# A hybrid encoder block on one Trainium2 core: two own buffers for the raw LoRA tile, and the first MLP slice's sums and squares on other engines

## The chip, the core and the metric

The kernel runs on one core of a Trainium2 chip. A core has five engines that run side by side and wait for each other through semaphores: TensorE (PE in the profile; its weight loads are shown apart as PEld), VectorE (DVE), ScalarE (ACT), GpSimd (POOL) and SyncE (SP). Each takes its instructions in a fixed order. Transfers between the chip's main memory and the on-chip memory (SBUF) are issued from the queue of an engine; in the kernel before, only SyncE and ScalarE issue any. TensorE writes to PSUM, from where VectorE and ScalarE read.

The metric is the time of one execution in microseconds (us). The kernel before has a median of 891.74 us over three runs (891.09 to 892.44). One execution was profiled; it took 891.46 us, and its span from the first to the last instruction is 889.7 us.

## What is computed

One layer of a streaming encoder, for 512 tokens and 16 learned meta tokens ahead of them, width 1024, all in float32:

```python
u = rmsnorm(h, norm_mix)
proj = u @ w_in
y_rw = rwkv7_branch(proj[..., :C_RW], ...)
y_fx = fox_branch(proj[..., C_RW:C_RW + C_FX], ...)
gates = sigmoid(proj[..., C_RW + C_FX:] + b_gate)
merged = gates[..., :1024] * (y_rw @ w_out_rw) + gates[..., 1024:] * (y_fx @ w_out_fx)
h = h + merged @ w_o
z = rmsnorm(h, norm_mlp)
h = h + square(relu(z @ w_up)) @ w_down
```

`rwkv7_branch` is a recurrence over the tokens; two of its inputs, the decay and the gate, go through small LoRA products (`w_lora_up`, `a_lora_up`, `g_lora_up`). `fox_branch` is causal attention with a forget gate. The MLP has 4096 hidden channels.

## The kernel before

**Precision.** A float32 operand is split into a high half (`whi`, a cast on ScalarE) and a low half (`wlo`, the difference, on VectorE or GpSimd), and each product is three passes: high by high, high by low, low by high. So every weight that is loaded costs a cast and a subtraction before TensorE can use it. `load_h` (lines 228 to 236) and `split` (268 to 270) do this; the raw weight tile `wraw`, `whi` and `wlo` have four buffers each, which is two blocks of weights.

**Who sets the order.** TensorE's order in the mixer (the recurrence, the attention and the input projections) is made by `Turns` and `Clock` (lines 62 to 183): several streams of work, each step with the time at which a cost model expects its inputs; the first stream that can go on is taken, and TensorE's instructions are kept in that order. The order of the other engines' instructions, and of the transfers in each queue, is made by the framework's own planner: it goes by the order of the program (work of the most urgent streams ahead of the rest) and by the times at which its cost model expects each instruction's inputs and buffers. On the chip, each queue is then worked off strictly in that order, whenever the inputs really come.

**The mixer** (up to about 450 us of the span) first loads the transposed input in two halves of four pieces (`xt`, lines 337 to 341), squares and sums it on TensorE (lines 351 to 359), and projects. Four pairs of heads follow. `load_lora` (lines 667 to 672) is called eight times: for each pair once in `decay` (line 699, part 0), and once at the start of each of the two `chain` streams per pair (line 887, part 1, used later in `group_norm`). It loads a raw tile `lraw`, 128 by 128, and splits it into `lw`. `lraw` carries the tag `yT`: it takes turns in one single buffer with `rkb` (line 764), `tmp` of the triangular inverse (line 829) and `yT` of the group norm (line 968).

**Between** lie the output projections, the residual, the second norm and the transposes of `z` (lines 1033 to 1131, until about 558 us).

**The MLP** runs in four slices of four channel pairs (`SLICES`, `FIRST`). In each slice:
- The up projection: 8 blocks of 24 matmuls (`up_part`, line 1139). After each block `up_evac` (line 1146) takes it out of PSUM: ScalarE computes `r = relu(po)`, VectorE `max(po, 0) * r`, which is the square. After every second block `left_factors` (line 1152) makes the seven left factors of a Strassen-Winograd product in `R`, each as a high half `fhi` (ScalarE) and a low half `flo` (VectorE).
- The right factors: for each pair, `factor_sums` (line 1179) loads four quarters of the down weight (`quarter`, line 1174, tile `traw` with three buffers, from SyncE's queue) and adds them on GpSimd to four sums T1 to T4; T2 needs T1, and T4 needs T2. The other three right factors are quarters themselves, loaded as `wraw`.
- Seven products (`product`, line 1240) of the left with the right factors, whose results VectorE and ScalarE add up. `fill` (line 1190) prepares the halves of the right factors ahead of them.

The first slice differs in its start: its first three blocks go in two halves of the tokens (lines 1214 to 1223), since the second half of `z` comes later.

Of the kernel before, what the change touches and what calls it, by code (L numbers as in the profile page):

```python
# [9 lines left out]
F32 = mybir.dt.float32  # L10
# [3 lines left out]
AF = mybir.ActivationFunctionType  # L14
ALU = mybir.AluOpType
# [171 lines left out]
def kernel(ctx, tc, ht, x, win, par, cst, gain, lora, wout, wo, wup, wdn, out, dbg=None):  # L187
    nc = tc.nc
    dbg = dbg or {}
    mm = nc.tensor.matmul  # L190
    act = nc.scalar.activation
    V, G, A = nc.vector, nc.gpsimd, nc.scalar
# [45 lines left out]
    def load_w(src, low=(V, V)):  # L238

        return [load_h(src[:, 512 * j:512 * j + 512], low[j], "w", (4, 4, 4)) for j in range(2)]  # L240
# [27 lines left out]
    def split(hi, lo, x):  # L268
        A.copy(hi, x)  # L269
        V.tensor_tensor(lo, x, hi.bitcast(F32), ALU.subtract)  # L270
# [6 lines left out]
    quarters = [[wdn[i][256 * c:256 * c + 256] for c in range(8)] for i in range(4)]  # L277

    with ExitStack() as st:
# [28 lines left out]
        rp = st.enter_context(tc.tile_pool(name="rp", bufs=1))  # L308
# [356 lines left out]
            return t[:, PADT:]  # L665

        def load_lora(p, part, bufs):
            raw = rp.tile([128, 128], F32, name="lraw", tag="yT")
            nc.sync.dma_start(raw, lora[p][:, 128 * part:128 * part + 128])
            lw = [wp.tile([128, 128], F32R, name=f"lw{part}{i}", bufs=bufs) for i in range(2)]  # L670
            split(lw[0], lw[1], raw)
            return lw
# [211 lines left out]
        def chain(g, prs):  # L884

            y = y_rw[:, 2 * g:2 * g + 2, :].rearrange("p a (b c) -> p a b c", c=64)
            lws = [load_lora(2 * g + pr_, 1, 2) for pr_ in range(2)]

            def ppy(name):
# [149 lines left out]
    def ppo():  # L1039
        return ps.tile([128, 512], F32, name="po")  # L1040
# [4 lines left out]
    with ExitStack() as st:  # L1045
# [7 lines left out]
        for m in range(KB):  # L1053
            w = load_w(wout[m])
            pp = []
            for br in range(2):
# [3 lines left out]
                po = ppo()  # L1060
# [21 lines left out]
        for j in range(2):  # L1082
            we = yp.tile([128, 2, 2, 512], F32R, name=f"we{j}", tag=("y_rw", "y_fx")[j])
            for x in range(2):
                raw = wp.tile([128, 512], F32, name="wraw", bufs=4)
# [11 lines left out]
        for k in range(KB):  # L1097
            raw = wp.tile([128, 512], F32, name="wraw", bufs=4)
# [9 lines left out]
        for i in range(4):  # L1108
            po = ppo()
# [26 lines left out]
    with ExitStack() as st:  # L1136
        dp = st.enter_context(tc.tile_pool(name="dp", bufs=1))

        def up_part(w, po, t0, t1):
            n = 0  # L1140
            for k in range(KB):
                for a, b in passes(wk(w, k), Z):
                    mm(po[:, t0:t1], a, b[:, k, t0:t1], start=n == 0, stop=n == 23)  # L1143
                    n += 1

        def up_evac(po, out):

            r = dp.tile([128, 512], F32, name="r", bufs=2)
            act(r, po, AF.Relu)
            V.scalar_tensor_tensor(out, po.rearrange("p (a b) -> p a b", b=256), 0.0, r.rearrange("p (a b) -> p a b", b=256), ALU.max, ALU.mult)  # L1150

        def left_factors(fhi, flo, j, R):

            def halves(a, b):
                A.copy(fhi[:, j, a:b], R[:, a:b])
                V.tensor_tensor(flo[:, j, a:b], R[:, a:b], fhi[:, j, a:b].bitcast(F32), ALU.subtract)

            halves(0, 3)
            a11, a12, s1, s2, s4 = (R[:, i, :] for i in (A11, A12, S1, S2, S4))
            V.tensor_tensor(R[:, S3:S1 + 1, :], R[:, 0:3:2, :], bc(R[:, 7, :], 1, 2), ALU.subtract)  # L1160
            V.tensor_tensor(s2, a11, s1, ALU.add)  # L1161
            V.tensor_tensor(s4, s2, a12, ALU.subtract)  # L1162
            halves(3, 7)

        A11, A12, A22, S3, S1, S2, S4 = range(7)
        B11, B12, B22, B21, T1, T2, T3, T4 = range(8)
# [4 lines left out]

        sums = {}

        def quarter(right, pair, pool=dp, name="traw", bufs=3):
            raw = pool.tile([128, 512], F32, name=name, bufs=bufs)
            nc.sync.dma_start(raw, quarters[right][pair // 2][128 * (pair % 2):128 * (pair % 2) + 128])
            return raw

        def factor_sums(p0, j):
            pair = p0 + j  # L1180
            b11, b12, b22, b21 = (quarter(x, pair) for x in (B11, B12, B22, B21))
            for x, c, d in (T1, b11, b12), (T3, b12, b22), (T2, T1, b22), (T4, T2, b21):
                t = dp.tile([128, 512], F32, name=f"t{x}{j}")
                G.tensor_tensor(t, sums[c, pair] if c in (T1, T2) else c, d, ALU.add)  # L1184
                sums[x, pair] = t

        def right_factor(right, pair):
            return sums[right, pair] if (right, pair) in sums else quarter(right, pair, wp, "wraw", 4)

        def fill(n):  # L1190

            while line and len(ready) < n:
                right, p, j = line.pop(0)
                raw = right_factor(right, p + j)
                hi = wp.tile([128, 512], F32R, name="whi", bufs=4)
                lo = wp.tile([128, 512], F32R, name="wlo", bufs=4)
                split(hi, lo, raw)
                ready.append((hi, lo))
# [10 lines left out]
        for p0, n_pairs in zip(FIRST, SLICES):  # L1209
# [3 lines left out]
            held, R = [], None  # L1213
# [6 lines left out]
            for n, b_ in enumerate(blocks):  # L1220
                if held:
                    w, po = held.pop(0)
                    up_part(w, po, 256, 512)
                else:
                    w = load_w(wup[b_])
                    po = ppo()
                    up_part(w, po, 0, 512)
                if n == 2 * n_pairs - 1:
                    fill(AHEAD)
                if n % 2 == 0:  # L1230
                    R = yp.tile([128, 8, 256], F32, name="R", tag=("y_rw", "y_fx")[n // 2 % 2])
                    up_evac(po, R[:, 0:8:7, :])
                else:
                    up_evac(po, R[:, 1:3, :])
                    left_factors(fhi, flo, n // 2, R)
                    factor_sums(p0, n // 2)

# [149 lines left out]
```

## Time and profile before

| | |
|---|---|
| median of three runs | 891.74 us (891.09 to 892.44) |
| profiled execution | 891.46 us |
| its span | 889.7 us |
| TensorE busy | 855.4 us, 96% of the span |
| VectorE, ScalarE, GpSimd busy | 632.1, 447.9, 246.0 us |
| mean TensorE clock granted | 0.987 of full speed |
| data moved | 95.90 MB, a mean of 108 GB/s |

How to read the rows in the next parts. A row of a group names line, engine, operation, `output<-inputs`, their shapes and the count; then busy time and mean ns of one; then the idle time of the engine just before these instructions, and after each `<-` what ended most of it. A row in order of time begins with start and duration in us; several instructions of one kind in a row are merged into one (`x2`), and the bracket holds the idle time before. A row of waits has the waiting engine and line, then who released it, and the total in us, the number of waits and the longest. A row of windows begins with the stretch and its length in us, then the busy time of PE, PEld, DVE, ACT and POOL with their counts, then the granted TensorE clock, the share of the transfer engines in use and GB/s; where a window is asked for one engine or one line, only its busy time is there. A queue of transfers is written SPq; its rows are the issues, not the transfers. TensorE's ends are modelled, so that its idle time is good to some hundredths of a microsecond.

### The profile page before, as it was taken

The page shows a single profiled execution, that of the slowest core. Times are in us where ns is not written, and L with a number is a line of the kernel's source. Part 1 is how long each engine was busy: PE and PEld are TensorE (multiplying, and loading weights), DVE is VectorE, ACT ScalarE, POOL GpSimd, SP SyncE. Part 2 cuts the span into 40 slices and gives each one's busy share as a digit, 9 for nine tenths or more (in the row PEclk, how much of TensorE's full clock was granted, in tenths as well). Part 3 has the DMA queues.
Part 4 walks back from the last instruction along what each step waited for, and adds up shares of the span by engine and source line. Part 5 has one row for each costly group of instructions (what it writes and reads, how often), then busy time and mean ns, then how long its engine had stood idle before and what let it go on. Part 6 is the DMA issues. An engine that isn't in the chain of part 4 may idle for free. (4 is left out here: it accounts for less than half of the span.)

```text
span 889.7 us, 15657 instructions
## 1 busy us (share of the span) xinstructions
PE 855.4 (96%) x5896; PEld 697.0 (78%) x5896; DVE 632.1 (71%) x1178; ACT 447.9 (50%) x927; POOL 246.0 (28%) x201
## 2 busy tenths in 40 slices
PE   7889899999999999999979999999999999999998
PEld 6878887778896787677758778978888888888886
DVE  6975896547878883565467655598687768877787
ACT  7747333865465533664464553246445434543552
POOL 1154443222353351112102200550640152046000
PEclk9999999999999999999979999999999999999999
DMA  6121114021121241212266550463564175326431
GB/s 215 52 93 48 49 39 150 2 89 56 51 65 52 65 137 56 78 50 72 65 220 196 183 180 11 131 193 91 171 209 108 51 230 159 118 70 226 117 97 71
DMA packets 52363, 95.90 MB, mean 108 GB/s; under 512 B 5816, under 2 KB 6968, under 8 KB 52288
## 3 DMA queue, kind: packets, MB, share of 16 engines
q1 hardware_dynamic: 49984, 90.71, 33.0%
q10 hardware_dynamic: 2304, 4.20, 1.3%
q8 instruction: 46, 0.75, 0.4%
q14 instruction: 29, 0.24, 0.1%
HBM read 88.57 MB, written 6.31 MB: 107 GB/s over the span
## 5 line engine op out<-in xcount | busy, mean ns | idle before, releaser
L497 PE MATMUL pj<-uhi,whi 128*128 128x264 f32 (+1 forms) x480 | 167.3, 348 | 0.0
L497 PE MATMUL pj<-ulo,whi 128*128 128x264 f32 (+1 forms) x480 | 155.6, 324 | 2.4 <-DVE ulo L400 2.4
L467 POOL TENSOR_TENSOR wlo<-wraw,whi 128x512 fp32r<-128x512 f32 x76 | 104.7, 1381 | 191.4 <-ACT whi L466 175.0
L497 PE MATMUL pj<-uhi,wlo 128*128 128x264 f32 (+1 forms) x480 | 155.2, 323 | 0.0
L497 PEld LDWEIGHTS pj<-uhi,whi 128*128 128x128 f32 x480 | 91.4, 191 | 20.4 <-issue 11.3
L1184 POOL TENSOR_TENSOR t<-traw 128x512 f32<-128x512 f32 x32 | 47.0, 1478 | 209.1 <-DVE wlo L270 132.0
L497 PEld LDWEIGHTS pj<-ulo,whi 128*128 128x128 f32 x480 | 91.8, 191 | 7.2 <-DVE ulo L400 2.9
L497 PEld LDWEIGHTS pj<-uhi,wlo 128*128 128x128 f32 x480 | 91.6, 191 | 7.1
L1143 PE MATMUL po<-zhi,wlo 128*128 128x512 f32 (+1 forms) x248 | 95.0, 383 | 1.6 <-DVE wlo L235 1.6
L235 DVE TENSOR_TENSOR wlo<-wraw,whi 128x512 fp32r<-128x512 f32 x88 | 75.8, 874 | 27.7 <-ACT whi L234 27.7
L1143 PE MATMUL po<-zhi,whi 128*128 128x512 f32 (+1 forms) x248 | 94.8, 382 | 0.0
L1143 PE MATMUL po<-zlo,whi 128*128 128x512 f32 (+1 forms) x248 | 94.8, 382 | 0.0
L234 ACT CAST whi<-wraw 128x512 fp32r<-128x512 f32 x88 | 53.5, 618 | 46.3 <-DMA wraw<-in_wup 27.8
L466 ACT CAST whi<-wraw 128x512 fp32r<-128x512 f32 x80 | 49.0, 619 | 41.3 <-PE pj L497 21.0
L1256 PE MATMUL po<-wlo,fhi 128*128 128x512 f32 x160 | 62.8, 392 | 0.2 <-DVE wlo L270 0.2
L1256 PE MATMUL po<-whi,flo 128*128 128x512 f32 x160 | 62.5, 390 | 0.0
L270 DVE TENSOR_TENSOR wlo<-t,whi 128x512 fp32r<-128x512 f32 x64 | 49.3, 784 | 18.5 <-ACT whi L269 17.6
L269 ACT CAST whi<-t 128x512 fp32r<-128x512 f32 x64 | 40.0, 625 | 44.1 <-DVE wlo L270 19.8
L1256 PE MATMUL po<-whi,fhi 128*128 128x512 f32 x160 | 62.0, 389 | 0.0
L1143 PEld LDWEIGHTS po<-zhi,wlo 128*128 128x128 f32 x248 | 46.6, 188 | 11.4 <-DVE wlo L235 2.4
L1143 PEld LDWEIGHTS po<-zlo,whi 128*128 128x128 f32 x248 | 46.6, 188 | 9.1
L1143 PEld LDWEIGHTS po<-zhi,whi 128*128 128x128 f32 x248 | 46.6, 188 | 8.9
(294 smaller groups left out, 1842.2 us busy)
## 6 DMA issues: line engine op xcount, KB each, us to landing
wraw<-in_win SPq DMA_DIRECT2D x84, 256.0 KB, 2.8
wraw<-in_wup SPq DMA_DIRECT2D x64, 256.0 KB, 3.6
traw<-in_wdn SPq DMA_DIRECT2D x64, 256.0 KB, 3.0
wraw<-in_wdn SPq DMA_DIRECT2D x48, 256.0 KB, 2.7
gd<-gt ACTq DMA_DIRECT2D x16, 256.0 KB, 2.0
wraw<-in_wout SPq DMA_DIRECT2D x16, 256.0 KB, 3.1
gl<-gd SPq DMA_DIRECT2D x16, 256.0 KB, 3.0
wraw<-in_wo SPq DMA_DIRECT2D x16, 256.0 KB, 3.0
```

The costliest lines, as they stand in the source:

```text
L234: A.copy(hi, raw)
L235: low.tensor_tensor(lo, raw, hi.bitcast(F32), ALU.subtract)
L269: A.copy(hi, x)
L270: V.tensor_tensor(lo, x, hi.bitcast(F32), ALU.subtract)
L466: A.copy(hi, raw)
L467: low.tensor_tensor(lo, raw, hi.bitcast(F32), ALU.subtract)
L497: mm(po, a, b[:, k, a0:a1], start=n == 0, stop=n == 23)
L1143: mm(po[:, t0:t1], a, b[:, k, t0:t1], start=n == 0, stop=n == 23)
L1184: G.tensor_tensor(t, sums[c, pair] if c in (T1, T2) else c, d, ALU.add)
L1256: mm(x[i], a[:, k, left, 128 * i:128 * i + 128], c, start=start and k == 0 and n == 0, stop=stop and k == n_pairs - 1 and n == 2)
```

## The change

The parts are these:
- `lraw` no longer shares the buffer of `yT`. It has two buffers of its own.
- `up_evac` gets a switch. In the first slice (`p0 == 0`) the square is computed on ScalarE from `r`; in the others on VectorE as before.
- `factor_sums` adds on VectorE in the first slice and loads its quarters from GpSimd's queue; in the other slices it adds on GpSimd and loads from SyncE's queue as before.
- `traw` has five buffers instead of three, in all slices.
- The scratch memory for transfer descriptors is set to 8192 bytes, which leaves room in SBUF for the added buffers.

```diff
         def load_lora(p, part, bufs):
-            raw = rp.tile([128, 128], F32, name="lraw", tag="yT")
+            raw = rp.tile([128, 128], F32, name="lraw", bufs=2)
             nc.sync.dma_start(raw, lora[p][:, 128 * part:128 * part + 128])
...
-        def up_evac(po, out):
+        def up_evac(po, out, by_act):
 
             r = dp.tile([128, 512], F32, name="r", bufs=2)
             act(r, po, AF.Relu)
-            V.scalar_tensor_tensor(out, po.rearrange("p (a b) -> p a b", b=256), 0.0, r.rearrange("p (a b) -> p a b", b=256), ALU.max, ALU.mult)
+            r = r.rearrange("p (a b) -> p a b", b=256)
+            if by_act:
+                act(out, r, AF.Square)
+            else:
+                V.scalar_tensor_tensor(out, po.rearrange("p (a b) -> p a b", b=256), 0.0, r, ALU.max, ALU.mult)
...
-        def quarter(right, pair, pool=dp, name="traw", bufs=3):
+        def quarter(right, pair, pool=dp, name="traw", bufs=5, queue=nc.sync):
             raw = pool.tile([128, 512], F32, name=name, bufs=bufs)
-            nc.sync.dma_start(raw, quarters[right][pair // 2][128 * (pair % 2):128 * (pair % 2) + 128])
+            queue.dma_start(raw, quarters[right][pair // 2][128 * (pair % 2):128 * (pair % 2) + 128])
             return raw
 
         def factor_sums(p0, j):
             pair = p0 + j
-            b11, b12, b22, b21 = (quarter(x, pair) for x in (B11, B12, B22, B21))
+            eng, queue = (V, G) if p0 == 0 else (G, nc.sync)
+            b11, b12, b22, b21 = (quarter(x, pair, queue=queue) for x in (B11, B12, B22, B21))
             for x, c, d in (T1, b11, b12), (T3, b12, b22), (T2, T1, b22), (T4, T2, b21):
                 t = dp.tile([128, 512], F32, name=f"t{x}{j}")
-                G.tensor_tensor(t, sums[c, pair] if c in (T1, T2) else c, d, ALU.add)
+                eng.tensor_tensor(t, sums[c, pair] if c in (T1, T2) else c, d, ALU.add)
                 sums[x, pair] = t
...
-                    up_evac(po, R[:, 0:8:7, :])
+                    up_evac(po, R[:, 0:8:7, :], p0 == 0)
                 else:
-                    up_evac(po, R[:, 1:3, :])
+                    up_evac(po, R[:, 1:3, :], p0 == 0)
...
-    nc = bacc.Bacc("TRN2", target_bir_lowering=False, num_devices=1)
+    nc = bacc.Bacc("TRN2", target_bir_lowering=False, num_devices=1, dynamic_dma_scratch_size=8192)
```

## The prediction

> **What bounds the kernel now.** I read the page's head first, then a table of windows cut at the stages of the MLP, then who waits for whom, then the order of time around the one gap that these show.
>
> ```profile
> span 889.7 us, 15657 instructions
> PE 855.4 (96%) x5896; PEld 697.0 (78%) x5896; DVE 632.1 (71%) x1178; ACT 447.9 (50%) x927; POOL 246.0 (28%) x201
> ```
>
> TensorE (PE) is busy for all but 889.7 - 855.4 = 34.3 us, so a change that takes no matmul away can win at most what it removes of those. The windows (stretch, length, then busy time of PE, weight loads, VectorE, ScalarE, GpSimd) say how much of them lies in the MLP:
>
> ```profile
> 553.80:601.40 47.60, 45.93 (x274) 40.50 (x273) 34.73 (x37) 17.57 (x30) 24.18 (x16) 1.00 0.52 155
> 601.40:640.00 38.60, 38.60 (x171) 31.84 (x170) 28.34 (x38) 20.48 (x33) 11.53 (x8) 1.00 0.38 110
> 640.00:683.26 43.26, 43.26 (x192) 35.83 (x191) 32.51 (x42) 20.11 (x32) 12.40 (x8) 1.00 0.58 176
> ```
>
> The first slice's up projection loses 47.60 - 45.93 = 1.67 us; its products and the second slice's up projection lose nothing. The second slice also gives PE's pace: 43.26 / 192 = 0.225 us a matmul, 24 x 0.225 = 5.4 us a block, 10.8 us a pair of blocks. The loss is one wait. In order of time:
>
> ```profile
> 578.22 2.31 DVE L1156 TENSOR_TENSOR flo<-R,fhi 128x1024 fp32r<-128x1024 f32 x1
> 579.41 3.96 POOL L1184 TENSOR_TENSOR t<-t,traw 128x512 f32<-128x512 f32 x2
> 587.47 1.51 DVE L1162 TENSOR_TENSOR R<-R 128x256 f32<-128x256 f32 x1
> 588.66 3.15 POOL L1184 TENSOR_TENSOR t<-t,traw 128x512 f32<-128x512 f32 x2
> 588.91 1.76 DVE L235 TENSOR_TENSOR wlo<-wraw,whi 128x512 fp32r<-128x512 f32 x1
> 590.59 2.31 DVE L1156 TENSOR_TENSOR flo<-R,fhi 128x1024 fp32r<-128x1024 f32 x1
> 590.72 0.50 PE L1143 MATMUL po<-zhi,wlo 128*128 128x512 f32 x1 [1.56 <-DVE wlo L235]
> 592.83 0.68 DVE L235 TENSOR_TENSOR wlo<-wraw,whi 128x512 fp32r<-128x512 f32 x1
> 597.88 0.42 DVE L1162 TENSOR_TENSOR R<-R 128x256 f32<-128x256 f32 x1
> 599.42 1.23 DVE L1156 TENSOR_TENSOR flo<-R,fhi 128x1024 fp32r<-128x1024 f32 x1 [0.52 <-ACT fhi L1155]
> 570.00:602.00 32.00, 31.16 (x32) 1.00 0.58 173
> ```
>
> The last row is VectorE alone: busy 31.16 of 32.00 us. The rows above it say why. While a GpSimd sum runs, the same VectorE instruction takes 1.76 instead of 0.68, 2.31 instead of 1.23, 1.51 instead of 0.42: about 1.08 us more each time. VectorE is late with a weight's low half, and PE waits 1.56 us for it. The loads have their share in it. The SyncE queue in the same stretch, and a line of the waits:
>
> ```profile
> 558.36 19.74 SPq L1176 DMA_DIRECT2D traw<-in_wdn  x12
> 578.15 0.42 SPq L231 DMA_DIRECT2D wraw<-in_wup  x1
> SPq L1176 <- POOL t L1184: 119.6, 56, 17.1
> ```
>
> Twelve loads of quarters take 19.74 us to issue, since their three buffers are freed by GpSimd's sums, and the next up-projection weight stands behind them until 578.15.
>
> **The change, part by part.** Durations from the groups:
>
> ```profile
> L1184 POOL TENSOR_TENSOR t<-t,traw 128x512 f32<-128x512 f32 x32 | 49.5, 1547 | 7.3 <-DMA traw<-in_wdn 6.3
> L1150 DVE SCALAR_TENSOR_TENSOR R<-po,r 128x512 f32<-128x512 f32 x32 | 21.9, 684 | 9.9 <-ACT r L1149 9.9
> L351 ACT ACTIVATE sq<-xt 128x528 f32<-128x528 f32 x8 | 5.1, 639 | 1.7 <-DMA xt<-in_ht 1.7
> 553.80:601.40 47.60, 10.15 (x8) 1.00 0.52 155
> traw<-in_wdn SPq DMA_DIRECT2D x64, 256.0 KB, 3.0
> ```
>
> *Sums to VectorE, square to ScalarE (first slice).* The fourth row is L235 alone: 10.15 us for 8, against 8 x 0.68 = 5.4 undisturbed, so 4.7 us of lengthening; the two 2.31 rows add 2 x 1.08 and the 1.51 row 1.09, together 8.0 us that I count. With no GpSimd sum there, VectorE's 34.73 us lose these 8.0 and eight squares (8 x 0.684 = 5.5) and gain 16 sums of 0.68 (10.9): 32.1 us in 47.6, or 8.0 a pair of blocks against PE's 10.8. There is room of 2.8 us a pair, and no instruction that is stretched. ScalarE takes 8 squares of 0.639 us (5.1): 17.57 becomes 22.7 of 47.6, in order behind its own Relu, where the square needs no other engine. PE's 1.67 us should go; I take 1.6. Bounds: 0 (another wait takes its place) and 1.67. If VectorE's room is gone, each sum of 0.68 us would be PE's.
>
> *Sixteen loads from SyncE to GpSimd's queue.* The trace has no GpSimd DMA. An issue is bounded below by the 0.33 us of a SyncE load and above by a sum of 1.547; I take the upper, nearer to work done on GpSimd itself: 16 x 1.547 = 24.8 us on an engine that has nothing else in the 47.6. It hides there. SyncE then goes straight to the up-projection weights; its other loads keep their order.
>
> *Quarters with five buffers instead of three, in every slice.* Later slices keep GpSimd and SyncE. PE loses nothing in them (43.26 of 43.26), so neither gain nor loss: 0.
>
> *The raw LoRA tile.* Until now it shares one buffer with the yT tiles, so its loads wait for whatever used that buffer, and stand in SyncE's queue:
>
> ```profile
> SPq L669 <- DVE AX L834: 16.7, 2, 10.8
> ACT lw L269 <- DMA lraw<-in_lora: 18.8, 7, 4.9
> 100.00:120.00 20.00, 20.00 (x172) 17.44 (x170) 16.27 (x39) 7.28 (x18) 4.12 (x5) 0.94 0.16 47
> 120.00:140.00 20.00, 19.99 (x111) 15.77 (x110) 17.64 (x24) 4.96 (x12) 8.53 (x6) 1.00 0.17 55
> ```
>
> SyncE stands 16.7 us and ScalarE 18.8 us for it. Most of that falls between 100 and 140 us, and there PE is busy 20.00 and 19.99 of 20.00: both stalls are covered by matmuls that were fed earlier. Removing them is worth 0 by these rows, and 0.2 at 230 us, where a LoRA subtraction stands in VectorE's queue (quoted below) and PE waits on that engine soon after. It costs something at the start:
>
> ```profile
> 0.74 0.39 SPq L669 DMA_DIRECT2D lraw<-in_lora  x1
> 1.65 1.37 SPq L338 DMA_DIRECT2D xt<-in_ht  x3
> 3.29 0.33 SPq L669 DMA_DIRECT2D lraw<-in_lora  x1
> 3.66 0.43 SPq L338 DMA_DIRECT2D xt<-in_ht  x1
> 230.62 0.29 DVE L270 TENSOR_TENSOR lw<-lraw,lw 128x128 fp32r<-128x128 f32 x1
> 5.07 0.64 ACT L351 ACTIVATE sq<-xt 128x528 f32<-128x528 f32 x1 [1.73 <-DMA xt<-in_ht]
> 5.76 5.09 PE L359 MATMUL pss<-sq,ones 128*128 128x264 f32 x12 [5.76 <-ACT sq L351]
> ```
>
> PE's first matmul waits for the first activations. The second LoRA load now waits for the first one's buffer and goes at 3.29. With two buffers it can go right behind the first, ahead of the activations: 0.33 to 0.39 us on the way to PE; a third one may take its place at 3.29. Bounds: -0.3 (the gap between 1.65 + 1.37 = 3.02 and 3.29 goes) and +0.8 (two loads ahead). I take +0.3.
>
> *Descriptor scratch 8192.* It moves no instruction of the trace: 0.
>
> Sum, against the profiled execution (891.46 us, of which 889.7 are the span): 891.46 - 1.6 - 0.2 + 0.3 = 889.96, so **890.0**. The median of before is 891.74, 0.3 above that execution.
>
> **The rivals.**
>
> *A gap more or less in the mixer.* With the LoRA work out of their places, the planner lays VectorE's, ScalarE's and SyncE's other work anew around 120 to 140, 224 to 232 and 315 to 320 us, while PE's order is written out and, I think, nearly the same. What a gap costs there (PE busy second, clock third from the end):
>
> ```profile
> 35.00:40.00 5.00, 3.19 (x26) 2.98 (x25) 5.00 (x11) 3.89 (x10) 1.65 (x2) 1.00 0.31 111
> 40.00:45.00 5.00, 4.38 (x23) 4.07 (x24) 4.87 (x9) 3.96 (x9) 1.24 (x2) 0.66 0.11 36
> 205.00:210.00 5.00, 4.41 (x52) 3.85 (x48) 4.55 (x16) 2.60 (x8) 2.56 (x2) 1.00 0.17 56
> 210.00:215.00 5.00, 3.94 (x30) 3.63 (x32) 2.62 (x7) 1.73 (x4) 1.42 (x1) 0.66 0.19 52
> ```
>
> From 35 to 45 us PE idles 1.81 + 0.62 us, and runs at 0.66 of its clock in the second half, which loses about 0.34 x 4.38 = 1.5 more: 3.9. From 205 to 215: 0.59 + 1.06, and 0.34 x 3.94 = 1.3: 3.0. A new stretch like the first gives 890.0 + 3.9 = **893.9**, slower; it decides from 3.6 us on, where it eats the gain and passes 0.2%. If the second one disappears: 890.0 - 3.0 = **887.0**. For it: these stretches are bound by the recurrence on VectorE, where the LoRA work stood. Against: that work is small (0.29 us a subtraction). TensorE: Matmul & The Clock Gate (HAM clock gate) of the Trainium skill lowers the clock after an idle window of about 3.4 us; the rows lower it after less. By the rule these gaps would cost their idle time alone, 892.4 and 888.4.
>
> *The stall only moves.* If the block's weight is late for its load or its turn on VectorE, not for the stretching, PE waits as before: 891.46 + 0.3 - 0.2 = **891.6**. Against it: VectorE's 32.1 us leave room, and SyncE is free.
>
> *VectorE blocked by the quarters.* Slower, by one mechanism: VectorE works in order, and its sums wait for transfers from a queue that the trace has never shown. Five buffers hold one set of four and one more, so three loads of the next set go only when a set's sums are done: 3 x 1.547 issue + 3.0 landing = 7.6 us. If the sums are queued ahead of the weights' low halves, VectorE stands so long at each of three changes; beyond the room, 3 x (7.6 - 2.8) = 14.4, less the one block (5.4) that is converted ahead: 9.0, **899.0**. It decides from waits of 2.8 + 5.4 / 3 = 4.6 us. Against it: VectorE's queue is planned with landing times, and nothing else holds up GpSimd. DMA: Bandwidth & Descriptors (Latency and other measured facts) of the Trainium skill speaks against the change here, with a first byte after about 1 us from this queue and 0.6 from SyncE's; no row here shows it, and by an estimate from it each wait grows by 0.4, the sum by 1.2 us in this rival only.
>
> **How the numbers follow.** Forecast 0.45, around 890.0 (888.8 to 891.2), half of it below 0.2% faster (889.96, from the median); a gap less 0.22; a gap more 0.18; the stall moves 0.08; VectorE blocked 0.07. Under 0.2% the measurement can hardly tell a change. Faster: 0.225 + 0.22 = 0.44; the same: 0.225 + 0.08 = 0.31; slower: 0.18 + 0.07 = 0.25. The range reaches to a gap less and a gap more with some room, 886.2 to 894.4, and leaves VectorE blocked out.
>
> **What would show it.** PE without an idle gap between 553 and 601 us; VectorE's instructions there at 0.68 and 1.23 us; VectorE busy near 32 us in that stage; GpSimd without sums before 610 us; the first matmul within 5.5 to 6.6 us. Wrong, if PE waits there for VectorE while VectorE waits for a quarter, if the stage keeps its 47.6 us, or if the mixer's end moves by more than 1 us either way.

## The result, and the profile after

The changed kernel takes **900.93 us** (median of eight runs, 897.45 to 901.85). The kernel before takes 891.41 us (median of eight). The ratio is 1.0075, with a 95% interval of 1.0054 to 1.0096: slower by 0.75%, where 890.0 and a small gain were forecast. The ratios here and below are taken over the fast runs of both kernels; the quotient of the two medians is 1.0107. The profiled execution took 897.62 us, the second fastest of the eight, so the two traces can show only 897.62 - 891.46 = 6.2 us of a loss that is 9.5 us between the medians.

```profile
span 895.9 us, 15657 instructions
PE 858.0 (96%) x5896; PEld 696.4 (78%) x5896; DVE 635.7 (71%) x1186; ACT 452.1 (50%) x935; POOL 234.9 (26%) x201
```

The span grew by 6.2 us. Cut at the stages, TensorE's work lies so:

| stage | before | after | difference |
|---|---|---|---|
| mixer (up to the first matmul of L1064) | 459.9 | 464.0 | +4.2 |
| from there to the first matmul of the MLP (L1143) | 93.9 | 93.5 | -0.4 |
| first slice, up projection | 47.64 | 45.91 | -1.73 |
| from the first product of a slice to that of the next, three times | 81.70, 81.88, 81.83 | 83.01, 83.26, 83.28 | +1.3, +1.4, +1.45 |
| rest | 42.73 | 42.76 | 0.0 |

**The first slice** did what was forecast. First its window (columns as before: length, PE, weight loads, VectorE, ScalarE, GpSimd, clock), then groups of VectorE and GpSimd in the stretch from 557 to 604 us, then one row of the waits:

```profile
557.52:603.43 45.91, 45.80 (x274) 40.60 (x272) 31.00 (x47) 22.10 (x38) 8.73 (x16) 1.00 0.58 179
...
L1189 DVE TENSOR_TENSOR t<-t,traw 128x512 f32<-128x512 f32 x8 | 5.5, 688 | 0.1
L1189 DVE TENSOR_TENSOR t<-traw 128x512 f32<-128x512 f32 x8 | 5.4, 689 | 8.2 <-DMA traw<-in_wdn 8.2
L235 DVE TENSOR_TENSOR wlo<-wraw,whi 128x512 fp32r<-128x512 f32 x8 | 5.4, 685 | 0.4 <-ACT whi L234 0.4
...
L1180 POOL DMA_DIRECT2D traw<-in_wdn x16 | 8.7, 548 | 58.5 <-DVE zlo L1131 50.3 <-DVE t L1189 7.6 <-issue 0.4
```

TensorE loses 0.11 us instead of 1.67, and no VectorE instruction is stretched: 685 ns for the low half of a weight. VectorE does wait 8.2 us for quarters, but TensorE doesn't notice. An issue on GpSimd's queue takes 548 ns.

**The mixer** loses at a place that the change doesn't touch: the eight copies of L845, in the triangular inverse, which the kernel runs twice, once for each two of the four pairs of heads. TensorE's matmuls come in the same order in both kernels, but for four near the start, so the delay can be followed from place to place (start, us):

| | before | after | difference |
|---|---|---|---|
| first inverse: its transposes begin (L836, VectorE) | 126.36 | 126.85 | +0.49 |
| first matmul of L851 on `Tt` behind it | 147.06 | 151.00 | +3.94 |
| second inverse: its transposes begin | 314.93 | 317.36 | +2.43 |
| first matmul of L851 on `Tt` behind it | 337.07 | 341.97 | +4.90 |
| first matmul of L1064 | 459.86 | 464.04 | +4.18 |

The two inverses cost 3.45 and 2.47 us, 5.9 together; 0.5 us was lost ahead of them, and 1.5 and 0.7 us came back between and behind them. In order of time around the first inverse, VectorE, GpSimd and SyncE's queue, in the kernel before:

```profile
129.51 0.65 DVE L845 COPY Tt<-TT 32x576 f32<-32x576 f32 x1
130.38 3.62 DVE L845 COPY Tt<-TT 32x576 f32<-32x576 f32 x3
134.01 3.81 DVE L845 COPY AX<-AX 32x576 f32<-32x576 f32 x4
...
131.12 1.62 POOL L467 TENSOR_TENSOR wlo<-wraw,whi 128x512 fp32r<-128x512 f32 x1
135.11 1.47 POOL L467 TENSOR_TENSOR wlo<-wraw,whi 128x512 fp32r<-128x512 f32 x1 [2.36 <-DMA wraw<-in_win]
...
98.26 17.30 SPq L453 DMA_DIRECT2D wraw<-in_win  x4
126.40 4.31 SPq L669 DMA_DIRECT2D lraw<-in_lora  x2
130.83 1.65 SPq L453 DMA_DIRECT2D wraw<-in_win  x2
```

and in the changed kernel:

```profile
129.99 5.50 DVE L845 COPY Tt<-TT 32x576 f32<-32x576 f32 x4
135.50 5.67 DVE L845 COPY AX<-AX 32x576 f32<-32x576 f32 x4
...
131.59 6.77 POOL L467 TENSOR_TENSOR wlo<-wraw,whi 128x512 fp32r<-128x512 f32 x4
138.66 1.34 POOL L467 TENSOR_TENSOR wlo<-wraw,whi 128x512 fp32r<-128x512 f32 x1 [0.30 <-ACT whi L466]
...
97.66 44.69 SPq L453 DMA_DIRECT2D wraw<-in_win  x12
```

Before, SyncE stood still until 126.40 for the LoRA tile's buffer. The weight loads behind it came late, so GpSimd had no more than two subtractions to do while VectorE copied. Now SyncE goes on loading, the weights are there, and GpSimd has subtractions to do through all of the copies. A copy takes 0.65 us alone and some 1.4 us on average here; the eight take 11.2 us (5.50 + 5.67) instead of 8.1 (0.65 + 3.62 + 3.81). TensorE waits for them (total, count, longest; both inverses), and loses clock on top (windows of PE alone, at the first inverse: busy time, then the granted clock):

```profile
PE pw L851 <- DVE AX L845: 4.5, 3, 1.9
...
136.00:140.00 4.00, 2.39 (x12) 1.00 0.56 173
140.00:145.00 5.00, 3.78 (x30) 0.71 0.59 176
```

It idles 1.61 and 1.22 us, and 0.29 x 3.78 = 1.1 us more go with the clock: 3.9. In the kernel before, the same two windows hold 0.01 and 0.02 us of idle time at the full clock, and the five microseconds behind them 0.66. The Trainium skill (TensorE: Matmul & The Clock Gate, HAM clock gate) has the clock go down after an idle window of about 3.4 us; here it went down after 2.8 us of idle time in two pieces.

The second inverse goes the same way: its copies take 11.2 us (5.51 + 5.71) instead of 10.1, and TensorE's wait for them grows from 0.73 us (first row, before) to 1.66 (second row, after), with the clock down behind it in the changed kernel and full in the kernel before:

```profile
328.40 0.91 PE L851 MATMUL pw<-AX,Bm 64*64 64x64 f32 x22 [0.73 <-DVE AX L845]
331.77 0.91 PE L851 MATMUL pw<-AX,Bm 64*64 64x64 f32 x22 [1.66 <-DVE AX L845]
330.00:335.00 5.00, 3.34 (x32) 0.82 0.34 104
335.00:340.00 5.00, 5.00 (x60) 0.84 0.31 108
```

What came back between the inverses is luck, and not the change's doing. Both kernels wait there for VectorE before L917, 1.65 us before and 1.64 after. Behind it the clock from 210 to 215 us was 0.66 in the kernel before (a row of the prediction), and in the changed kernel's execution it stayed full:

```profile
210.00:215.00 5.00, 3.36 (x33) 1.00 0.28 78
```

One kernel does both: e3 and e15 below have the same code and the same wait, and a clock of 1.00 and of 0.69 in that stretch.

**The later slices** each begin late. SyncE's queue and ScalarE at the start of the second slice's up projection, before:

```profile
627.57 6.92 SPq L1176 DMA_DIRECT2D traw<-in_wdn  x5
634.58 0.38 SPq L231 DMA_DIRECT2D wraw<-in_wup  x1
...
637.56 0.62 ACT L234 CAST whi<-wraw 128x512 fp32r<-128x512 f32 x1 [2.11 <-DMA wraw<-in_wup]
```

and after, with TensorE's two waits:

```profile
629.51 8.84 SPq L1180 DMA_DIRECT2D traw<-in_wdn  x7
638.44 0.86 SPq L231 DMA_DIRECT2D wraw<-in_wup  x2
...
641.36 0.62 ACT L234 CAST whi<-wraw 128x512 fp32r<-128x512 f32 x1 [3.97 <-DMA wraw<-in_wup]
...
642.03 0.50 PE L1143 MATMUL po<-zhi,whi 128*128 128x512 f32 x1 [0.32 <-ACT whi L234]
643.24 0.50 PE L1143 MATMUL po<-zhi,wlo 128*128 128x512 f32 x1 [0.47 <-DVE wlo L235]
```

With five buffers the planner puts seven quarter loads ahead of the slice's first up-projection weight, where it put five before. The first of them is issued 7.01 us ahead of that weight before (634.58 - 627.57), and 8.93 us after (638.44 - 629.51). The weight comes 1.9 us later, and TensorE, which lost nothing here before, waits twice, in each of three slices. The idle time is 0.32 + 0.47 us; by their starts the two matmuls come 0.70 and 0.87 us behind the one ahead, where 0.23 is the pace, so that most of the 1.3 us is here.

### The profile page after: what moved, and what is told of

Its sections match the earlier page's. It is cut to its first block, busy times and chain, and to the rows that moved or that the text cites. A ratio compares the mean times of both kernels' runs of the same rounds, so it can differ in the third digit from the quotient of the medians.

```text
span 895.9 us, 15657 instructions
## 1 busy us (share of the span) xinstructions
PE 858.0 (96%) x5896; PEld 696.4 (78%) x5896; DVE 635.7 (71%) x1186; ACT 452.1 (50%) x935; POOL 234.9 (26%) x201
## 4 chain that ended last, share of the span: by engine, by line
PE 70%; DVE 19%; DMA 4%; ACT 4%; issue 3%; POOL 0%; SPq 0%; ACTq 0%; DVEq 0%; POOLq 0%
PE po L1143 20%; PE pj L497 18%; PE po L1261 8%; PE pd L1261 4%; PE po L1113 2%; PE po L1064 2%; DVE wlo L270 2%; DMA wraw<-in_wup 2%; PE pw L851 2%; PE psr L784 1%; PE psc L603 1%; DVE AX L845 1%; PE py L648 1%; DVE tmp L833 1%; DVE Tt L845 1%
## 5 line engine op out<-in xcount | busy, mean ns | idle before, releaser
L1143 PE MATMUL po<-zhi,wlo 128*128 128x512 f32 (+1 forms) x248 | 95.3, 384 | 1.4 <-DVE wlo L235 1.4
L1143 PE MATMUL po<-zhi,whi 128*128 128x512 f32 (+1 forms) x248 | 95.2, 384 | 1.0 <-ACT whi L234 1.0
L1143 PE MATMUL po<-zlo,whi 128*128 128x512 f32 (+1 forms) x248 | 94.8, 382 | 0.0
L1189 POOL TENSOR_TENSOR t<-traw 128x512 f32<-128x512 f32 x24 | 36.3, 1527 | 162.5 <-DVE wlo L270 162.1
L270 DVE TENSOR_TENSOR wlo<-t,whi 128x512 fp32r<-128x512 f32 x64 | 52.6, 834 | 18.9 <-ACT whi L269 18.0
L1143 PEld LDWEIGHTS po<-zhi,wlo 128*128 128x128 f32 x248 | 46.6, 188 | 12.0 <-DVE wlo L235 3.0
L1143 PEld LDWEIGHTS po<-zhi,whi 128*128 128x128 f32 x248 | 46.6, 188 | 11.1 <-ACT whi L234 2.3
L1143 PEld LDWEIGHTS po<-zlo,whi 128*128 128x128 f32 x248 | 46.6, 188 | 8.9
```

Of the source, the lines that this page charges most:

```text
L1189: eng.tensor_tensor(t, sums[c, pair] if c in (T1, T2) else c, d, ALU.add)
```

## The experiments

Theory A: the LoRA tile's own buffers set SyncE free, GpSimd's subtractions move beside VectorE's copies, and these hold up TensorE. Theory B: five quarter buffers put more loads ahead of the first up-projection weight. Rivals: the new first slice costs by itself; the LoRA work costs where the planner puts it; the quarters' transfers or VectorE's waits for them cost. e1 to e16 were timed in five rounds against the kernel before on the same chip:

| kernel | median, us | ratio to before | 95% interval |
|---|---|---|---|
| changed kernel | 900.93 | 1.0075 | 1.0054 to 1.0096 |
| e1: LoRA tile shared again | 894.30 | 1.0007 | 0.9983 to 1.0032 |
| e2: three quarter buffers again | 896.21 | 1.0024 | 0.9998 to 1.0051 |
| e3: both, the first slice's edits alone | 888.85 | 0.9947 | 0.9919 to 0.9976 |
| e4: before, with the LoRA buffers alone | 900.33 | 1.0076 | 1.0050 to 1.0102 |
| e5: changed, SyncE made to wait | 897.65 | 1.0059 | 1.0029 to 1.0088 |
| e6: changed, four copies on ScalarE | 906.14 | 1.0147 | 1.0115 to 1.0179 |
| e7: e3, four copies on ScalarE | 903.03 | 1.0120 | 1.0077 to 1.0162 |
| e8: before, with five quarter buffers alone | 893.78 | 1.0017 | 0.9992 to 1.0042 |
| e9: changed, GpSimd held during the copies | 896.60 | 1.0051 | 1.0033 to 1.0070 |
| e10: changed, quarters off SyncE's queue | 896.74 | 1.0051 | 1.0029 to 1.0074 |
| e11: e3, GpSimd held (by the tile `tmp`) | 894.46 | 1.0028 | 1.0007 to 1.0050 |
| e12: e11, quarters off SyncE's queue | 895.23 | 1.0048 | 1.0026 to 1.0070 |
| e13: changed, e9 and e10 together | 890.49 | 0.9978 | 0.9957 to 1.0000 |
| e14: e3, GpSimd held (by a tile of its own) | 889.55 | 0.9962 | 0.9942 to 0.9982 |
| e15: e3 again | 889.46 | 0.9950 | 0.9929 to 0.9972 |
| e16: changed kernel again | 900.38 | 1.0084 | 1.0052 to 1.0116 |

e1 to e4 share a chip and its runs of the kernel before (median 892.81), as do e5 to e8 (893.07), e9 to e12 (892.38; the chip of e5 to e8) and e13 to e16 (894.22).

### The parts of the change: e1, e2, e3, e4

```diff
# e1, and e3
-            raw = rp.tile([128, 128], F32, name="lraw", bufs=2)
+            raw = rp.tile([128, 128], F32, name="lraw", tag="yT")
# e2, and e3
-        def quarter(right, pair, pool=dp, name="traw", bufs=5, queue=nc.sync):
+        def quarter(right, pair, pool=dp, name="traw", bufs=3, queue=nc.sync):
# e4, on the kernel before, with the small descriptor scratch
-            raw = rp.tile([128, 128], F32, name="lraw", tag="yT")
+            raw = rp.tile([128, 128], F32, name="lraw", bufs=2)
```

> The changed kernel with the raw LoRA tile back in the buffer of yT; everything else of the change stays. By stages of the two traces the changed kernel loses 4.1 us in the mixer and 4.1 us in the second to fourth MLP slice, and wins 1.7 us in the first slice. Theory 1 (the LoRA buffers cost the mixer its 4.1 us): the mixer ends as before, at 460 us, and the time is before + 2.4 us (ratio about 1.003). Rival (the mixer's loss comes from another part, or from a state of the run): the mixer still ends near 464 us and the time stays at before + 6 us.

> The changed kernel with three buffers for the quarters instead of five; everything else of the change stays. Theory 3 (five buffers let two more quarters stand ahead of a slice's first up weights in SyncE's queue): each of the later slices takes 81.8 us again instead of 83.2, the time falls by 4.1 us to before + 2.4 (ratio about 1.003). Rival theory 4 (the later slices lose for what the first slice's sums or queue leave behind): they stay at 83.2 us. The first slice, without its two more buffers, keeps its 1.7 us if VectorE has room to wait for quarters, and loses up to that if not.

> Only the first slice's edits: sums on VectorE, quarters from GpSimd's queue, square on ScalarE, with three buffers for quarters and the raw LoRA tile in the buffer of yT. Theories 1 and 3: mixer and later slices as before, the first slice 1.7 us shorter: before - 1.7 (ratio about 0.998). If the losses come from the first slice's edits: before + 2 to + 6.

> The kernel before with only the raw LoRA tile's two buffers (and the smaller descriptor scratch). Theory 1: VectorE's eight copies of line 845 take about 11.2 us in each of the two inverses against 8.1 and 10.0 before, since SyncE no longer stands still and GpSimd gets its weights earlier and runs its subtractions against them; the mixer ends 4 us later, the time is before + 4 (ratio about 1.0045). Theory 2 (the loss needs the other edits): before, within 0.2%.

e3 shows that the first slice's edits are a gain of their own: 0.9947 to the kernel before, and 0.9950 on another chip (e15). Both buffer edits cost. By the ratios of one chip, the LoRA buffers cost 1.0024 - 0.9947 = 0.77% or 6.9 us (e2 over e3), and the quarter buffers 1.0007 - 0.9947 = 0.60% or 5.4 us (e1 over e3); e4, the LoRA buffers with nothing else, costs 0.76%. Each loss is where its theory puts it: with the shared LoRA tile the copies of the first inverse are back at 0.65 + 3.62 + 3.79 us (e1), with three quarter buffers the later slices take 81.62, 81.82 and 81.83 us (e2). e1's profiled execution, 898.22 us, doesn't show the gain in its mixer: it was 3 us late before the inverse began, and the copies of its second inverse took 11.1 us although the tile is shared. e3 also has the small descriptor scratch, which therefore isn't what costs.

### Five quarter buffers alone: e8

```diff
# on the kernel before, with the small descriptor scratch
-        def quarter(right, pair, pool=dp, name="traw", bufs=3):
+        def quarter(right, pair, pool=dp, name="traw", bufs=5):
```

> The kernel before, with five buffers for the quarters and nothing else of the change (and the small descriptor scratch). Theory: the seven quarter loads that then stand ahead of a slice's first up weight in SyncE's queue make that weight 2 us later, so the three later slices go from 81.8 to about 83.1 us each, +4 us in all, the mixer stays as before, and the time is 4 to 6 us over the kernel before of the same chip. Rival D (five buffers cost only together with the new first slice): the slices stay at 81.8 and the time within 1 us of before.

The slices went as expected, to 82.97, 83.31 and 83.25 us, so the buffers cost there whatever the first slice does. The total did not: 1.0017, about nothing, where 4 to 6 us were expected. Of the 4.1 us, 1.2 came back in the old first slice (46.44 us instead of 47.64), perhaps because five buffers hold its quarters up less, which wasn't followed up, and 1.5 ahead of the MLP, in an execution whose clock stayed full at 210 us, which by e3 and e15 is luck. The buffers' price stands out where the first slice is already mended, as in e1 over e3.

### What makes the copies long: e5, e9, e6

```diff
# e5, ahead of the LoRA tile in load_lora
+            hold = rp.tile([128, 128], F32, name="hold", tag="yT")
+            nc.sync.dma_start(hold, lora[p][:, 128 * part:128 * part + 128])
# e9, behind the loop of the copies
+            G.tensor_copy(tmp[96:128, :1], Dn[96:128, 0, 32:33])
# e6, and e7 on e3
-                    V.tensor_copy(dst[rs_, :, o:o + 32], src[rs_, :, :n2].rearrange("p t n -> p n t"))
+                    (A.copy if src is At else V.tensor_copy)(dst[rs_, :, o:o + 32], src[rs_, :, :n2].rearrange("p t n -> p n t"))
```

> The changed kernel, with one unused load more for each LoRA part: it goes into the buffer that the LoRA tile had before and stands on SyncE's queue ahead of the LoRA load itself, so SyncE again has to wait for that buffer while the LoRA tiles keep buffers of their own. Theory A (SyncE's stand-still kept the later weight loads, and with them GpSimd's subtractions of L467, out of the way of VectorE's copies of L845): the eight copies of the first inverse take about 8.1 us again and not 11.2, the first L1064 stands some 4 us earlier than in the changed kernel (about 460), the slices stay at 83.0 to 83.3 us, and the time is near that of e1, 894 (892 to 897). Rival B (the own buffers cost by themselves, by where the planner then puts the LoRA work): the copies stay at 11.2 us, and the time stays at 900 (898 to 903).

SyncE waited again, until 127.58 us, and the first inverse's copies took 4.49 + 4.78 = 9.3 us: shorter than the 11.2 of the changed kernel, longer than the expected 8.1. GpSimd still had three subtractions beside the last four copies. TensorE nonetheless lost nothing at the first inverse any more (20.75 us in the table below, 20.70 before), which is theory A's first half: with SyncE's stall back, the loss there is gone. The second inverse kept copies of 11.2 us and lost 0.95 us (23.10 against 22.15). The median, 897.65, lies between what the theories gave; why it stays above e1's isn't shown.

> The changed kernel with one tiny GpSimd copy more for each of the two inverses: it reads an element that the last of VectorE's eight copies of L845 writes, so GpSimd stands still from its next subtraction on until the copies are done. The order of the instructions on TensorE, VectorE, ScalarE and SyncE is the same as in the changed kernel. Theory A (GpSimd's subtractions beside VectorE's copies are what lengthens them, and TensorE waits for them): the eight copies take about 8 us and not 11.2 in both inverses, TensorE's waits on L845 fall from 4.5 us to about 1, the first L1064 stands 3 to 5 us earlier than the changed kernel's (459 to 461), the slices stay at 83.0 to 83.3, and the time is 3 to 6 us under 900.9, 895 to 898. Rival (the earlier weight loads cost by themselves, the copies only cover it): the copies shorten, GpSimd's work comes late in their place, and the time stays within 2 us of 900.9.

This is the direct test: the order on TensorE, VectorE, ScalarE and SyncE stays that of the changed kernel, and only GpSimd stands still. VectorE in order of time, both inverses:

```profile
130.39 4.50 DVE L845 COPY Tt<-TT 32x576 f32<-32x576 f32 x4
134.90 2.83 DVE L845 COPY AX<-AX 32x576 f32<-32x576 f32 x4
...
318.59 4.49 DVE L845 COPY Tt<-TT 32x576 f32<-32x576 f32 x4
323.09 2.85 DVE L845 COPY AX<-AX 32x576 f32<-32x576 f32 x4
```

The second group of four runs while GpSimd stands and takes 2.83 us, 0.7 a copy, instead of 5.67. TensorE's waits on L845 are gone from the list, its windows from 120 to 160 us lose 1.07 us at the full clock instead of 2.83 with a dip, the first L1064 stands at 460.9 instead of 464.0, and the MLP starts 4.2 us earlier. The median is 4.3 us under that of the changed kernel, from other runs; by the ratios it is 0.24%, 2.1 us, with intervals that overlap. What carries the test is its trace, and e13 below, timed beside the changed kernel on one chip. The slices stay at 83.0 to 83.3. So it is the subtractions beside the copies that hold TensorE up. The Trainium skill (SBUF — State Buffer, Who interferes with whom) has VectorE and GpSimd share a pair of ports, which one instruction holds for its whole length while the other waits; a copy needs the pair only in VectorE's two-port modes. Which mode these copies ran in no run shows; that they are lengthened beside GpSimd the rows show.

From the start of an inverse's transposes (L836) to the first matmul of L851 on `Tt`, us, in the profiled executions:

| kernel | first inverse | second inverse |
|---|---|---|
| before; LoRA tile shared: e1, e3, e8, e15 | 20.70; 21.17, 20.82, 20.88, 20.77 | 22.15; 23.18, 22.14, 22.12, 24.75 |
| changed; own buffers too: e2, e4, e10, e16 | 24.16; 24.16, 25.61, 24.18, 25.64 | 24.61; 24.61, 24.62, 24.60, 23.08 |
| own buffers, SyncE made to wait: e5 | 20.75 | 23.10 |
| own buffers, GpSimd held: e9, e13 | 20.71, 20.54 | 22.70, 22.69 |

At the first inverse the kernels of the table part without exception. At the second they don't quite: e15, with the tile shared, loses as much as the changed kernel, and e16, the changed kernel again, loses less.

> The changed kernel, with those copies of L845 that read the tile At given to ScalarE; the others stay on VectorE. Nothing else is changed. Theory A (VectorE's copies are slowed by GpSimd's subtractions that run beside them): the copies that stay on VectorE keep 1 us or more each when GpSimd subtracts beside them, but those on ScalarE run beside them, so that the group ends 3 us or more earlier than the 11.2 us of the changed kernel, the first L1064 stands 3 to 8 us earlier for the two inverses, and the time is 893 to 897. Rival C (something else in the mixer takes the time, and the long copies only cover it): the copies end earlier, but TensorE waits elsewhere for as long, and the time stays within 2 us of 900.9.

A miss, and an ill-chosen test. The planner laid the mixer's order anew, TensorE's too, and ScalarE, which works in order, was put in front of a fill of GpSimd's that the copies need (ScalarE in order of time):

```profile
132.18 4.95 ACT L845 COPY AX<-AX 32x576 f32<-32x576 f32 x4 [6.68 <-POOL AX L840]
```

It stood 6.68 us there with its casts behind it. The kernel is some 5 us slower than the changed one; about the theory it says nothing, since the order is another.

### The later quarters off SyncE's queue: e10

```diff
-            eng, queue = (V, G) if p0 == 0 else (G, nc.sync)
+            eng, queue = (V if p0 == 0 else G, G)
```

> The changed kernel with the quarters of the three later slices issued on GpSimd's queue too, as those of the first slice are; their sums stay on GpSimd, and five buffers stay. The order on TensorE, VectorE and ScalarE is the same as in the changed kernel. Theory B (seven quarters ahead of a slice's first up weight in SyncE's queue make it late): the first up weight is issued 4 us or more earlier, TensorE's waits on L234 and L235 at the slices' starts go, the three later slices take 81.6 to 81.9 us each and not 83.0 to 83.3, and the time is about 4 us under 900.9, 896 to 898. Rival (the quarters' transfers themselves, or VectorE's waits, make the slices longer): the slices stay at 83, and the time at 900 to 902.

The direct test of theory B, with TensorE, VectorE and ScalarE in the order of the changed kernel. The first products of the four slices in the chain of waits, the changed kernel:

```profile
603.59 16.34 PE po L1261 x72
686.60 16.50 PE po L1261 x72
769.86 16.50 PE po L1261 x72
853.14 16.50 PE po L1261 x72
```

and e10:

```profile
604.87 16.34 PE po L1261 x72
686.49 16.50 PE po L1261 x72
768.46 16.55 PE po L1261 x72
850.28 16.51 PE po L1261 x72
...
635.48 31.23 SPq L231 DMA_DIRECT2D wraw<-in_wup  x16
```

From one to the next are now 81.62, 81.97 and 81.82 us, 4.1 less in all, and the median is 4.2 us under that of the changed kernel (other runs; by the ratios 2.1 us, with intervals that overlap). The last row is SyncE's queue: nothing but up-projection weights, the first one at 635.48 instead of 638.44, though this slice begins 1.3 us later. The five buffers, the transfers and the sums are the same, so it was the order in SyncE's queue. In every trace but e6's, whose order is another, the slices go by this alone: 81.6 to 82.4 us each with three buffers or with the quarters on GpSimd's queue, 83.0 to 83.3 with five on SyncE's.

### Is that all of it: e13, e15, e16

e13 has the edits of e9 and e10; e15 is e3 and e16 the changed kernel, on e13's chip.

> The changed kernel with both cures, the GpSimd stand-still of e9 and the quarter queue of e10. If the two losses are separate stretches of the kernel, the gains add: the copies take 7.3 us in both inverses, the first L1064 stands near 461, the slices take 81.6 to 82.0 us, and the time is 8 to 9 us under the changed kernel's, 892 to 893. If there is a third loss in the change, it is what then still lies over e3 of this chip: 3 us or more would call for one. Rival: the two gains are one (a shift that either brings): 895 to 897.

> e3 once more on this chip, as the measure for e13 and e14: 887 to 891, 2 to 5 us under the kernel before.

> The changed kernel once more on this chip, as the measure for e13: 898 to 903, 5 to 9 us over the kernel before.

Both cures together bring 9.9 us by the medians of one chip (890.49 against 900.38), and 1.06% or 9.5 us by the ratios, clear of the noise. Alone, e9 and e10 gave 4.3 and 4.2 by the medians, so the gains add; by the ratios they gave 2.1 each, so how nearly they add isn't settled by the times. By the stretches in the traces they do: 5.4 us at the inverses and 4.1 in the slices. Above e15 remain 1.0 us by the medians (890.49 - 889.46) and 0.28% or 2.5 us by the ratios, whose intervals overlap. The two places account for nearly all of the loss; a third one of 2 or 3 us isn't excluded.

### A version that beats both: e3, and e7, e11, e12, e14 on top of it

```diff
# e11 and e12, as in e9
+            G.tensor_copy(tmp[96:128, :1], Dn[96:128, 0, 32:33])
# e14
+            G.tensor_copy(rp.tile([128, 2], F32, name="hold", bufs=1)[96:128, :1], Dn[96:128, 0, 32:33])
```

e12 has the edit of e10 too.

> e3 (only the first slice's sums on VectorE and its square on ScalarE, LoRA tile and quarters as before) with the copies of L845 that read At on ScalarE. Theory A: in e3 the copies take 8.1 and 10.1 us, and part of that is GpSimd's doing; with half of them on ScalarE the two groups end 3 us or so earlier each, and the time is 883 to 887. Rival C: TensorE isn't waiting for the group as a whole, or ScalarE's copies come late behind its other work: 888 to 890, as e3.

> e3 (only the first slice's sums on VectorE and its square on ScalarE) with the GpSimd stand-still of e9. Theory A: e3's copies take 8.1 and 10.1 us, the second group falls to about 8, and the time is 0 to 3 us under e3's 888.85, 886 to 889. Rival: TensorE has other waits there, 888 to 891.

> e11 with the later quarters on GpSimd's queue as in e10, and three buffers. Theory B: with three buffers the later slices already take 81.6 to 81.8 us without a wait, so nothing is left to win there, and the time is that of e11 within 1 us. Rival: VectorE and GpSimd wait longer for quarters that GpSimd issues itself, and the slices take up to 1 us more each: 889 to 892.

> e11 with the tiny copy going into a tile of its own and not into the tile tmp, for whose buffer the LoRA load waits. Theory A: e11 lost its 5 us because that load, and SyncE's queue behind it, then waited for the tiny copy; with a tile of its own SyncE is free at about 127 us as in e3, the copies take 7.3 us in both inverses against 8.1 and 10.1, and the time is 0 to 3 us under e3's. Rival (a stand-still of GpSimd costs as much as it brings here): e3's time or up to 3 us over it.

None beats e3. e7 failed like e6. e11 and e12 are misses of the edit's own making: the tiny copy writes into `tmp`, and in e3 the LoRA load waits for the buffer of `tmp`. SyncE's queue in e11:

```profile
123.47 0.33 SPq L453 DMA_DIRECT2D wraw<-in_win  x1
137.81 0.33 SPq L669 DMA_DIRECT2D lraw<-in_lora  x1
```

SyncE stood until 137.81 instead of 126.88, and TensorE lost 5.0 us between 140 and 160. e12 is within 1 us of e11, as expected. In e14 SyncE goes on at 126.37 and both inverses' copies take 7.1 us; e15's take 8.1 and 11.1. Yet the medians are the same, 889.55 and 889.46. So long copies do not cost by themselves. What costs is that they grow past what TensorE has to do meanwhile: at the first inverse 8.1 us are covered and 11.2 are not; at the second e3's 10.1 us leave TensorE a wait of 0.7 us, e15's 11.1 one of 1.8.

## Why the prediction was wrong, point by point

- **The first slice: right.** -1.73 us against the -1.6 taken. VectorE is busy 31.0 us there (32.1 worked out), ScalarE 22.1 (22.7). The GpSimd issue was bounded by 0.33 and 1.547 us and taken at the upper end; it is 0.548, so the 16 take 8.7 us and not 24.8. Hidden either way. The medians give the edits more, 4.0 us (e3) and 4.8 (e15). The stage they mend is not always as short as in the profile of before: the same code took 50.3 us in e4's.
- **The start: right in sign.** The LoRA loads go out as a pair ahead of the activations, and the first matmul starts at 5.86 instead of 5.76: +0.1 against +0.3. The gain of 0.2 at 230 us isn't seen: TensorE idles 2.13 us from 220 to 240, and idled 2.17.
- **"Quarters with five buffers ... neither gain nor loss: 0": wrong, +4.1 us in the trace.** The step argued that TensorE lost nothing in those slices. That shows there is nothing to gain; it doesn't show there is nothing to lose. SyncE's queue was read in the first slice, where twelve quarter loads hold back a weight, but not in the later ones, where five stand ahead of one and little of the cover was left (the cast at 637.56 had waited 2.11 us for that load): 1.9 us more ahead of it cost 1.3 to 1.45 us a slice. More buffers let more loads stand in front.
- **"Both stalls are covered ... removing them is worth 0": wrong, +4.2 us in the trace, 6.9 by e2 over e3.** That TensorE was fed is true of SyncE's first stand-still, up to 126 us; the second, up to 315 us, was counted in the 16.7 us but its windows weren't read. What the stalls kept apart wasn't asked: with SyncE free, GpSimd gets weights earlier, beside VectorE's copies. The prediction had priced this very collision in the first slice (1.08 us for each VectorE instruction beside a GpSimd one) and not looked for it where SyncE's stalls end. Its own sign of being wrong, the mixer's end moving by more than 1 us, came true: 4.2.
- **The rival "a gap more in the mixer" came nearest.** Its price of 3.9 us is what the stretch from 136 to 145 us lost, an agreement by luck, since it was read off another stretch. Its cause was put elsewhere, in the LoRA work itself, which is small (0.29 us); the large thing that moved was the weight loads behind it in SyncE's queue. That it was thought unlikely follows from this. And there were two places in the mixer, one at each inverse, and the slices besides.
- **The rival "a gap less": its stretch at 205 to 215 us did lose its dip**, in the profiled execution, for 1.5 us. That isn't the change's doing either, as e3 and e15 show.
- **"VectorE blocked by the quarters": its wait exists** (8.2 us) and is hidden, as argued.

The LoRA buffers cost 6.9 us by the runs and 4.2 by the two profiled executions, and most of that gap is the clock. The two inverses cost 5.9 us in the changed kernel's execution, 7.4 in e4's (25.61 - 20.70 and 24.62 - 22.15) and 5.9 in e16's; the 4.2 holds, with them, the 1.5 us that the kernel before had lost by chance at 210 us. The mixer's length varies between executions of one kernel: e16's profiled execution took 903.04 us with copies of the same 11.2 us, and was 3.2 us behind that of the changed kernel already when the inverse's transposes began (130.02 against 126.85); its clock was 0.74 from 100 to 120, against 0.89. Open is what decides whether the clock drops behind a wait, and whether the buffers make such dips likelier.

## What to carry to other kernels

A stall that nobody waits for may still keep two engines apart: before removing it, follow the queue behind it to the first instructions that it sets free, and see what runs beside them. A deeper buffer is not free either, even with room for it: here it let the planner put more loads of one kind ahead of another kind in the same queue, so read what stands behind them and how much of its time is left. And undo the parts of a change one by one; here the part that was worth having was hidden under two that cost more.

## What the runs showed of the hardware

- A VectorE copy of 32 by 576 elements with one input takes 0.65 to 0.70 us alone and up to 1.72 us while GpSimd works beside it, 1.07 us longer; the operations of the old first slice grew by about 1.08.
- The granted clock of a stretch differs between executions of one kernel. From 100 to 120 us, with TensorE busy throughout, it was 0.89 in the changed kernel's first profile and 0.74 in e16's, 0.15 x 20 = 3 us apart; the idle time from 80 to 100 us was the same (2.90 and 2.91 us), that from 60 to 80 was not (0.23 and 2.36), but there the clock stood the other way (0.91 and 1.00).
- The same wait of 1.65 us is followed by a lower clock in one execution and not in another of the same kernel: 1.00 in e3 and 0.69 in e15 from 210 to 215 us.
- An issue of a 256 KB load takes GpSimd 0.55 us on its queue, where SyncE's takes 0.33 to 0.44.
